# Running sums of the seven products in PSUM, with fewer VectorE additions and another order of items

## Chip, core and metric

The kernel runs on one core of a Trainium2 chip. The metric is the device time of one execution in microseconds (us). The engines are TensorE (PE, with its weight loads shown as PEld), VectorE (DVE), ScalarE (ACT), GpSimd (POOL) and SyncE (SP), which issues most of the DMAs.

## The reference

A decoder trunk of two layers on 256 rows of width 2048: each layer has an attention (differential attention in the first, multi-head latent attention in the second), a cross-attention into 256 memory rows, and an MLP with squared ReLU, each behind an RMSNorm and with a residual addition. One RMSNorm closes the trunk. The part that the change touches is the MLP:

```python
def sq_relu_mlp(h, wup, wdown):
    return jnp.square(jax.nn.relu(h @ wup)) @ wdown   # h 256 x 2048, wup 2048 x 8192, wdown 8192 x 2048

x = x + sq_relu_mlp(rms_norm(x, mlp_norm[i]), mlp_wup[i], mlp_wdown[i])
```

## The kernel before

**Products in halves.** Every float32 operand is split into a high half (a cast to float32r) and a low half (the rest). One product of the algorithm is three matmuls: high by high, high by low, low by high. Weights come from HBM as tiles `raw` of 128 x 2048 (1 MB, seven buffers). A tile is split in two steps of 128 x 1024: ScalarE casts the high half (`whi`, L199) and VectorE subtracts to get the low half (`wlo`, L200), with four buffers of each. TensorE's 128 x 512 matmuls (L157) take these as the moving operand.

**The MLP's items.** The hidden width 8192 is worked in eight blocks (b = 0 to 7) of 1024 columns. The 256 rows are two tiles of 128. Block 0 is multiplied straightforwardly: *up* items. The hidden activations (after ReLU, square and transposes) meet wdown in *down* items, whose sums stay in four PSUM banks. An up or down item is one weight tile with 24 matmuls.

Blocks 1 to 7 are multiplied as a 2 x 2 block product in seven products instead of eight (class `Seven`, Strassen's scheme). The 2 x 2 blocks are the two row tiles by the two halves of the inner width, and the two halves of the inner width by two groups of 512 columns. p1 to p7 each multiply one form of the activations (a quarter of it, or a running sum `s1`, `s2`, `s3`, `s4` of quarters) by one form of the weights. A product has two items (x = 0 and x = 1), each one weight tile with 12 matmuls, and sums into one PSUM bank, `pr`. The weight forms are made in place: additions of two raw tiles on VectorE (L824, at the items of p5, p6 and p2), and for p7 an accumulating DMA from GpSimd's queue (L816), which adds a tile from HBM onto p3's raw tile once p3's item has been split. p7's x-th item needs the tile that followed p3's x-th item.

**Combination before.** After the second item of each product its bank is read. p1 and p5 are copied to SBUF by ScalarE (L892). The others are combined by VectorE in SBUF (helper `add`, L886): p6 + p1; p3 + p5 and from that minus p6; p2 + p1; p7 onto p6 and p5 minus that; p4 onto p6. These are seven VectorE operations a block, five from PSUM and two within SBUF. Each of the four results goes to `out`: ReLU with the row's scale and square on ScalarE (L1212, L1213), then four transposes on TensorE (L161) through a side bank and a split into the hidden unit (L338, L339).

**What sets the order.** TensorE's instructions run in the order in which they are written. `mlp_line` writes it: it merges the list `rest` (up and down items) with the list `seven` by a running balance of estimated VectorE time (function `vector`) against TensorE time (1 for a Seven item, 2 for another), with share the ratio of the two sums; a Seven item is taken when the balance is at or below zero, or when the next down item's hidden units are not ready. Within a block `ORDER` gives the items. In blocks 5 to 7 the line before is p1 p1 p5 D p5 D p6 D p3 p6 D p3 p2 D D p7 p2 D p7 D p4 p4, with D for a down item; block 1 is p1 p1 p5 U p5 U p6 U p3 p6 U p3 p2 p7 p2 D D D p7 D D p4 p4, with U for an up item.

The other engines' instructions are ordered by a scheduler that works from estimated times and priorities at build time; `urgent()` raises a priority. Weight tiles are fetched up to four items ahead (`take`, `fill`), and the loads of p5, p6 and p2 one item earlier still (`fetch`). PSUM has eight banks in one pool.

Of the kernel before, what the change touches and what calls it, by code (L numbers as in the profile page):

```python
# [10 lines left out]
F32 = mybir.dt.float32  # L11
# [3 lines left out]
ALU = mybir.AluOpType  # L15
AX = mybir.AxisListType

P = 128
# [3 lines left out]
CH = 512  # L22
# [5 lines left out]
EVS = 7  # L28
# [19 lines left out]
def trunk(ctx, tc, x, xT, xT0, mem, memT, positions, gcols, gfinal, lam_vecs, consts, W, out):  # L48
    nc = tc.nc

    def pool(name, bufs, space=None):
        kw = {"space": space} if space else {}
        return ctx.enter_context(tc.tile_pool(name=name, bufs=bufs, **kw))
# [5 lines left out]
    work = pool("work", 2)  # L59
# [5 lines left out]
    def nm(s):  # L65
        serial[0] += 1
        return f"{s}_{serial[0]}"
# [4 lines left out]
    def bank(tag="ax"):  # L72
        return banks.tile([P, CH], F32, tag="bank", name=nm(tag))
# [38 lines left out]
    def pump():  # L112
        while True:
            now = [t for t in side if t.due() <= clock[0]]
            if not now:
                return
            min(now, key=lambda t: (t.ready, t.serial)).step()

    def need(tasks):
        for task in tasks:  # L120
            while not task.done:
                nxt = min(side, key=lambda t: (t.due(), t.serial))
                clock[0] = max(clock[0], nxt.due())
                nxt.step()
# [24 lines left out]
    def give_back():  # L149
        free_banks[0] += 1  # L150

    def mmul(o, stationary, moving, start, stop):
        n = 1
        for d in moving.shape[1:]:
            n *= d
        clock[0] += max(0.11, n / 2400 + 0.0133)
        return nc.tensor.matmul(o, stationary, moving, start=start, stop=stop)  # L157

    def flip(o, src):
        clock[0] += 0.109  # L160
# [5 lines left out]
    def urgent():  # L166

        return tc.high_priority(offset=URGENT)
# [58 lines left out]
    def take():  # L227
        fill()
        got = ready.pop(0)
        fill()  # L230
        taken[0] += 1
        if taken[0] in hooks:
            hooks[taken[0]]()
        return got

    def unit_part(o, a, h, hi, lo, t, first, last):

        width = o.shape[-1]
        for k in range(2):
            kk = 2 * h + k  # L240
            ah, al = a.get(0, kk, t), a.get(1, kk, t)
            wh = hi[:, k * width : (k + 1) * width]
            wl = lo[:, k * width : (k + 1) * width]
            mmul(o, ah, wh, first and kk == 0, False)
            mmul(o, ah, wl, False, False)
            mmul(o, al, wh, False, last and kk == 3)
        pump()
# [534 lines left out]
    class Chunk:  # L782
# [11 lines left out]
        def items(self):  # L794
            return [Item(self, u, [job]) for u, job in enumerate(self.all)]
# [5 lines left out]
    class Seven:  # L801

        ORDER = "p1 p1 p5 p5 p6 p3 p6 p3 p2 p7 p2 p7 p4 p4".split()
        A = {"p1": (0, 0), "p2": (0, 1), "p3": "s4", "p4": (1, 1), "p5": "s1", "p6": "s2", "p7": "s3"}

        def __init__(self, l, b):
# [54 lines left out]
        def items(self):  # L863
            order = [(p, self.ORDER[:i].count(p)) for i, p in enumerate(self.ORDER)]
            return [Item(self, u, [self.job(*u)]) for u in order]

        def products(self, a, u, copied, out):
            p, x = u
            form = a.form(self.A[p])
            need(form.tasks)  # L870
            if x == 0:
                self.banks[p] = bank("pr")
            o = self.banks[p]
            for h, (hi, lo) in enumerate(take()):
                for k in range(2):
                    kk = 4 * x + 2 * h + k
                    wh, wl = (w[:, k * CH : (k + 1) * CH] for w in (hi, lo))
                    mmul(o, form[:, 0, kk], wh, kk == 0, False)
                    mmul(o, form[:, 0, kk], wl, False, False)
                    mmul(o, form[:, 1, kk], wh, False, kk == 7)  # L880
                pump()
            if x == 0:
                return

            def add(o, p, q, op=ALU.add):
                nc.vector.tensor_tensor(o, p, q, op)  # L886

            c = copied
            if p in ("p1", "p5", "p6", "p3"):
                c[p] = work.tile([P, CH], F32, tag="ev", name=nm(p), bufs=EVS)  # L890
            if p in ("p1", "p5"):
                nc.scalar.copy(c[p], o)  # L892
            elif p == "p6":
                add(c[p], o, c["p1"])
            elif p == "p3":
                add(c[p], o, c["p5"])
                add(c[p], c[p], c["p6"], ALU.subtract)
                out(0, 1, c[p], c[p])
            elif p == "p2":
                add(c["p1"], o, c["p1"])  # L900
                out(0, 0, c["p1"], c["p1"])
            elif p == "p7":
                add(c["p6"], o, c["p6"])
                add(c["p5"], c["p5"], c["p6"], ALU.subtract)
                out(1, 1, c["p5"], c["p5"])
            else:
                add(c["p6"], o, c["p6"])
                out(1, 0, c["p6"], c["p6"])

    def mlp_line(l):  # L910

        def up(b, h):
            return Chunk(l, "up", [(b, h)]).items()

        def both(b, *more):
            return [(b, 0), (b, 1), *more]

        groups = [both(b) for b in range(MLP_BLOCKS)]  # L920

        def down(i):

            end = len(groups) - 1
            pairs = ((0, 1), (2, 3)) if (end - i) % 2 == 0 else ((2, 3), (0, 1))
            chunks = [Chunk(l, "down", groups[i], c, open=i == 0) for c in pairs[0]]
            chunks += [Chunk(l, "down", groups[i], c, close=i == end) for c in pairs[1]]
            return [i for c in chunks for i in c.items()]

        line = up(0, 0)  # L930
        rest = up(0, 1) + [i for b in range(MLP_BLOCKS - 1) for i in down(b)]
        seven = [i for b in SEVEN for i in Seven(l, b).items()]

        def vector(item):

            if isinstance(item.of, Seven):
                p, x = item.u
                return 1 + (p in ("p5", "p6", "p2")) + x * {"p6": 0.3, "p3": 0.9, "p2": 0.6, "p7": 0.9, "p4": 0.6}.get(p, 0)
            return 1 + 0.6 * (item.u == len(item.of.all) - 1 and item.of.close)

        def tensor(item):
            return 1 if isinstance(item.of, Seven) else 2

        rest, after = rest[:-3], rest[-3:]

        share = sum(map(vector, rest + seven)) / sum(map(tensor, rest + seven))
        usable = {(0, 0): 0}
        lead, now = 0.0, 0
        while rest or seven:
            of = rest[0].of if rest else None  # L950
            late = rest and of.kind == "down" and any(usable.get(h, math.inf) > now for h in of.halves)
            take_seven = seven and (not rest or late or lead <= 0)
            item = (seven if take_seven else rest).pop(0)
            lead += vector(item) - share * tensor(item)
            now += tensor(item)
            line.append(item)
            if isinstance(item.of, Seven):
                if item.u == ("p4", 1):
                    usable.update({(item.of.b, h): now + 6 for h in range(2)})
            elif item.of.kind == "up" and item.u == 3:  # L960
                usable[item.of.halves[0]] = now + 4
        return line + after, down(len(groups) - 1)
# [586 lines left out]
def build(a, w):  # L1549
    import concourse.bacc as bacc  # L1550

    nc = bacc.Bacc("TRN2", target_bir_lowering=False, num_devices=1, dynamic_dma_scratch_size=1024)
    arrays = {}

    def dram(name, v):
        arrays[f"in_{name}_dram"] = v
        return nc.dram_tensor(f"in_{name}_dram", v.shape, mybir.dt.from_np(v.dtype), kind="ExternalInput").ap()

    args = [dram(k, a[k]) for k in ("x", "xT", "xT0", "mem", "memT", "positions", "gcols", "gfinal", "lam_vecs", "consts")]
    weights = {k: dram(k, v) for k, v in w.items()}  # L1560
    o = nc.dram_tensor("out_0_dram", (S, D), F32, kind="ExternalOutput").ap()
    with tile.TileContext(nc, schedule_with_timeline_sim=True) as tc, tc.manual_schedule(engines={mybir.EngineType.PE}):
        trunk(tc, *args, weights, o)
    return nc, arrays
# [8 lines left out]
```

## Time and profile before

| | before |
|---|---|
| timed runs, median of 3 | 2216.66 us (2216.47 to 2217.68) |
| profiled execution, first to last instruction (its span) | 2214.3 us |
| the median of the timed runs above that span | 2.4 us |
| TensorE busy | 2201.7 us |
| VectorE busy | 1760.7 us |
| ScalarE busy | 1357.0 us |
| mean granted TensorE clock | 0.999 |

No time of its own is given for the profiled execution besides its span; the timed runs stand beside it. In rows of the profile L157 is line 157, the helper that writes every matmul, so rows are told apart by tiles: `mm` is the bank of an up or down item, `pr` that of a Seven item, `ax` a side bank of transposes. `out<-in` names the tile written and those read, xcount is the number of instructions, and a bracket at the end of a timeline row has the idle time of that engine just before the instruction and what ended it. "Busy, mean ns | idle before" are the columns of a group.

### The profile page before, as it was taken

The numbers are of one execution on the slowest core, as the hardware profiler recorded it, in microseconds if no ns is written. First come the engines' busy times: TensorE is split into PE (matmuls) and PEld (weight loads), VectorE is DVE, ScalarE is ACT, GpSimd is POOL, SyncE is SP. The second block draws the span as 40 slices with busy tenths as digits, with TensorE's granted clock in tenths as the row PEclk, the third lists the DMA queues.
The fourth block names the chain that finished last, engine by engine and source line by source line (L and its number), as shares of the span: only waits on it lengthen the run. The fifth ranks groups of instructions, "written<-read, shape, count | busy, mean of one in ns | idle before, by whom it ended". The sixth has DMA issues, their size and how long they took to land.

```text
span 2214.3 us, 27594 instructions
## 1 busy us (share of the span) xinstructions
PE 2201.7 (99%) x10559; PEld 1846.1 (83%) x10559; DVE 1760.7 (80%) x1961; ACT 1357.0 (61%) x1811; POOL 134.3 (6%) x222
## 2 busy tenths in 40 slices
PE   9999999999999999999999999999999999999998
PEld 7888888888888888888889988888888888888886
DVE  6665757779889889889765878778988998898874
ACT  7554546666666666666655755556766666666664
POOL 1111010000000000000000411000000000000001
PEclk9999999999999999999999999999999999999999
DMA  9446555436766766875845444634767667677681
GB/s 386 156 152 228 188 194 210 166 118 209 259 203 211 254 212 215 250 218 212 251 176 178 136 152 163 247 129 156 222 234 228 210 246 228 197 259 226 195 282 57
DMA packets 69683, 454.73 MB, mean 205 GB/s; under 512 B 7984, under 2 KB 8368, under 8 KB 17584
## 3 DMA queue, kind: packets, MB, share of 16 engines
q1 hardware_dynamic: 65232, 423.09, 53.6%
q0 software_dynamic: 4032, 29.36, 7.2%
q8 instruction: 82, 1.34, 0.2%
q10 hardware_dynamic: 288, 0.52, 0.1%
q14 instruction: 49, 0.40, 0.0%
HBM read 450.85 MB, written 2.10 MB: 205 GB/s over the span
## 4 chain that ended last, share of the span: by engine, by line
PE 93%; DVE 4%; issue 1%; ACT 1%; POOL 1%; DMA 1%; POOLq 0%; ACTq 0%; DVEq 0%
PE mm L157 65%; PE pr L157 23%; PE ax L157 2%; PE ax L161 2%; DVE wlo L200 2%; PE mm L161 1%; DVE raw L824 1%; DVE unit L440 0%; DVE raw L468 0%; POOL rs L382 0%; ACT whi L199 0%; DMA raw<-in_mlp_wup_dram 0%; DVE raw L451 0%; DMA raw<-in_da_wqkv_dram 0%; DVE x L496 0%
## 5 line engine op out<-in xcount | busy, mean ns | idle before, releaser
L199 ACT CAST whi<-raw 128x1024 fp32r<-128x1024 f32 (+2 forms) x962 | 1000.4, 1041 | 715.2 <-PE mm L157 590.6
L200 DVE TENSOR_TENSOR wlo<-raw,whi 128x1024 fp32r<-128x1024 f32 (+2 forms) x962 | 1147.8, 1209 | 344.9 <-ACT whi L199 329.6
L157 PE MATMUL mm<-whi,unit 128*128 128x512 f32 (+3 forms) x4416 | 1396.2, 388 | 0.4 <-ACT unit L370 0.4
L157 PEld LDWEIGHTS mm<-whi,unit 128*128 128x128 f32 x4416 | 825.2, 188 | 161.4 <-ACT unit L370 1.5
L157 PE MATMUL mm<-wlo,unit 128*128 128x512 f32 (+3 forms) x2208 | 851.5, 386 | 1.0 <-DVE wlo L200 1.0
L157 PE MATMUL pr<-whi,unit 128*128 128x512 f32 x1568 | 505.6, 391 | 0.0
L157 PEld LDWEIGHTS mm<-wlo,unit 128*128 128x128 f32 x2208 | 415.3, 188 | 79.2 <-DVE wlo L200 3.3
L157 PEld LDWEIGHTS pr<-whi,unit 128*128 128x128 f32 x1568 | 294.4, 188 | 61.0
L157 PE MATMUL pr<-wlo,unit 128*128 128x512 f32 x784 | 305.4, 390 | 0.6 <-DVE wlo L200 0.6
L824 DVE TENSOR_TENSOR raw<-raw,raw 128x2048 f32<-128x2048 f32 x84 | 192.1, 2287 | 26.1 <-DMA raw<-in_mlp_wup_dram 25.6
L157 PEld LDWEIGHTS pr<-wlo,unit 128*128 128x128 f32 x784 | 147.3, 188 | 31.5 <-DVE wlo L200 1.4
L496 DVE TENSOR_TENSOR x<-x,mm 128x512 f32<-128x512 f32 x152 | 100.3, 679 | 9.4 <-PE mm L157 9.0
L816 POOL DMA_DIRECT2D raw<-in_mlp_wup_dram x28 | 24.6, 879 | 1094.7 <-DVE wlo L200 1094.7
L382 POOL TENSOR_TENSOR rs<-rs,mhalf 128x1 f32<-128x1 f32 (+1 forms) x28 | 26.0, 932 | 649.3 <-DVE rs L381 649.3
L338 ACT CAST unit<-ax 128x512 fp32r<-128x512 f32 x64 | 37.2, 581 | 24.4 <-PE ax L161 24.4
L886 DVE TENSOR_TENSOR p<-pr,p 128x512 f32<-128x512 f32 x70 | 47.9, 684 | 2.6 <-PE pr L157 2.6
L157 PE MATMUL mm<-unit,whi 128*128 128x256 f32 x256 | 47.1, 285 | 0.1
L161 PE MATMUL ax<-identr,p 128*128 128x128 f32 x304 | 46.2, 272 | 0.5 <-ACT unit L1434 0.5
L161 PEld LDWEIGHTS ax<-identr,p 128*128 128x128 f32 x304 | 37.7, 139 | 10.8 <-ACT unit L1434 0.9
L1212 ACT ACTIVATE p<-p,r 128x512 f32<-128x512 f32 x56 | 40.3, 720 | 9.3 <-DVE p L886 9.2
L339 DVE TENSOR_TENSOR unit<-ax,unit 128x512 fp32r<-128x512 f32 x64 | 43.7, 683 | 1.6 <-ACT unit L338 1.1
L376 ACT ACTIVATE junk<-x 128x512 bf16<-128x512 f32 x56 | 35.2, 628 | 9.4 <-DVE x L496 8.4
(161 smaller groups left out, 1053.2 us busy)
## 6 DMA issues: line engine op xcount, KB each, us to landing
raw<-in_mlp_wup_dram SPq DMA_DIRECT2D x128, 1024.0 KB, 5.0
raw<-in_mlp_wdown_dram SPq DMA_DIRECT2D x128, 1024.0 KB, 5.1
raw<-in_da_wqkv_dram SPq DMA_DIRECT2D x45, 1024.0 KB, 7.3
raw<-in_mlp_wup_dram POOLq DMA_DIRECT2D x28, 1024.0 KB, 8.1
raw<-in_da_wo_dram SPq DMA_DIRECT2D x16, 1024.0 KB, 5.0
raw<-in_ca_wkv_dram SPq DMA_DIRECT2D x16, 1024.0 KB, 5.0
raw<-in_mla_wo_dram SPq DMA_DIRECT2D x16, 1024.0 KB, 5.2
raw<-in_ca_wq_dram SPq DMA_DIRECT2D x8, 1024.0 KB, 6.9
```

What stands on the lines that cost most here:

```text
L157: return nc.tensor.matmul(o, stationary, moving, start=start, stop=stop)
L161: nc.tensor.transpose(o, src, ident)
L199: nc.scalar.copy(hi, r)
L200: nc.vector.tensor_tensor(lo, r, f32(hi), ALU.subtract)
L338: nc.scalar.copy(hi, src)
L339: nc.vector.tensor_tensor(dst[:, 1, :n, t * P : (t + 1) * P], src, f32(hi), ALU.subtract)
L376: nc.scalar.activation(junk[:, : src.shape[1]], src, AF.Square, accum_out=acc)
L382: nc.gpsimd.tensor_tensor(r[:, :n], r[:, :n], mhalf.broadcast_to([P, n]), ALU.pow)
L496: nc.vector.tensor_tensor(xc, xc, ps, ALU.add)
L824: nc.vector.tensor_tensor(o, o, q, ALU.add)
L886: nc.vector.tensor_tensor(o, p, q, op)
L1212: nc.scalar.activation(r, src, AF.Relu, scale=rstd[t])
```

## The change

The products that share a sum are accumulated in one bank. p1, p6, p7 and p4 go onto p1's bank one after the other, p3 onto p5's, and p2 has its own. After p1, p5 and p6 ScalarE copies the running sum to SBUF, with raised priority. VectorE does three operations a block: the sum with p3 minus the copy made after p6, the copy of p5 minus the sum with p7 (with raised priority), and p2 plus the copy of p1. p4's result is read from PSUM by the ReLU. A matmul that goes onto a used bank does not start a new sum (`start` is false), and has to come after the reading of that bank's earlier sum.

In `ORDER` the last items of p2 and p7 change places: p2 p7 p7 p2 for p2 p7 p2 p7. The planner's estimates of VectorE's time (`vector`) get values for the three operations, which changes where down items are put among the Seven items.

```diff
-    def mmul(o, stationary, moving, start, stop):
+    def mmul(o, stationary, moving, start, stop, onto=False):
...
-        return nc.tensor.matmul(o, stationary, moving, start=start, stop=stop)
+        return nc.tensor.matmul(o, stationary, moving, start=start, stop=stop, skip_group_check=onto)
...
-        ORDER = "p1 p1 p5 p5 p6 p3 p6 p3 p2 p7 p2 p7 p4 p4".split()
+        ORDER = "p1 p1 p5 p5 p6 p3 p6 p3 p2 p7 p7 p2 p4 p4".split()
+        ONTO = {"p1": "p1", "p6": "p1", "p7": "p1", "p4": "p1", "p5": "p5", "p3": "p5", "p2": "p2"}
...
-            if x == 0:
+            onto = self.ONTO[p]
+            if x == 0 and onto == p:
                 self.banks[p] = bank("pr")
-            o = self.banks[p]
+            o = self.banks[onto]
...
-                    mmul(o, form[:, 0, kk], wh, kk == 0, False)
-                    mmul(o, form[:, 0, kk], wl, False, False)
-                    mmul(o, form[:, 1, kk], wh, False, kk == 7)
+                    mmul(o, form[:, 0, kk], wh, kk == 0 and onto == p, False, onto != p)
+                    mmul(o, form[:, 0, kk], wl, False, False, onto != p)
+                    mmul(o, form[:, 1, kk], wh, False, kk == 7, onto != p)
...
-            def add(o, p, q, op=ALU.add):
-                nc.vector.tensor_tensor(o, p, q, op)
+            def kept():
+                t = work.tile([P, CH], F32, tag="ev", name=nm(p), bufs=EVS)
+                with urgent():
+                    nc.scalar.copy(t, o)
+                return t

             c = copied
-            if p in ("p1", "p5", "p6", "p3"):
-                c[p] = work.tile([P, CH], F32, tag="ev", name=nm(p), bufs=EVS)
-            if p in ("p1", "p5"):
-                nc.scalar.copy(c[p], o)
-            elif p == "p6":
-                add(c[p], o, c["p1"])
+            if p in ("p1", "p5", "p6"):
+                c[p] = kept()
             elif p == "p3":
-                add(c[p], o, c["p5"])
-                add(c[p], c[p], c["p6"], ALU.subtract)
-                out(0, 1, c[p], c[p])
+                nc.vector.tensor_tensor(c["p6"], o, c["p6"], ALU.subtract)
+                out(0, 1, c["p6"], c["p6"])
+            elif p == "p7":
+                with urgent():
+                    nc.vector.tensor_tensor(c["p5"], c["p5"], o, ALU.subtract)
+                out(1, 1, c["p5"], c["p5"])
             elif p == "p2":
-                add(c["p1"], o, c["p1"])
+                nc.vector.tensor_tensor(c["p1"], o, c["p1"], ALU.add)
                 out(0, 0, c["p1"], c["p1"])
-            elif p == "p7":
-                add(c["p6"], o, c["p6"])
-                add(c["p5"], c["p5"], c["p6"], ALU.subtract)
-                out(1, 1, c["p5"], c["p5"])
             else:
-                add(c["p6"], o, c["p6"])
-                out(1, 0, c["p6"], c["p6"])
+                out(1, 0, o, work.tile([P, CH], F32, tag="ev", name=nm(p), bufs=EVS))
...
-                return 1 + (p in ("p5", "p6", "p2")) + x * {"p6": 0.3, "p3": 0.9, "p2": 0.6, "p7": 0.9, "p4": 0.6}.get(p, 0)
+                return 1 + (p in ("p5", "p6", "p2")) + x * {"p3": 0.6, "p2": 0.6, "p7": 0.6, "p4": 0.3}.get(p, 0)
```

## The prediction

> **What bounds the kernel now.** I read the page first, then the busy time by stretches, then the waits of TensorE (PE), and then the timeline around each wait that was left. The two MLPs lie roughly in the stretches 505 to 1175 us and 1540 to 2215 us.
>
> ```profile
> span 2214.3 us, 27594 instructions
> PE 2201.7 (99%) x10559; PEld 1846.1 (83%) x10559; DVE 1760.7 (80%) x1961; ACT 1357.0 (61%) x1811; POOL 134.3 (6%) x222
> ...
> 505.00:1175.00 670.00, 669.12 (x3027) 553.51 (x3026) 573.95 (x528) 425.81 (x477) 13.46 (x17) 1.00 0.68 221
> ...
> 1540.00:2215.00 675.00, 664.84 (x2990) 548.96 (x2988) 568.10 (x517) 421.51 (x470) 24.31 (x24) 1.00 0.66 215
> ```
>
> The rows of stretches give length, then busy time of PE, PEld, DVE (VectorE), ACT (ScalarE) and POOL. In the first MLP PE is busy for 669.12 of 670.00 us; VectorE, which the change relieves, for 573.95 (86%). A busy PE can still be a slow one, because ends of matmuls are modelled. So the pace comes from the chain of waits: one row of 24 products without a wait in it,
>
> ```profile
> 546.67 5.44 PE pr L157 x24
> ```
>
> 5.44 / 24 = 0.227 us for one 128x512 product, hence 2.72 us for one item of a Seven block (12 products) and 5.44 us for an up or down item (24). The change leaves the number of products as it is, so only the time that PE loses beyond this pace can be won. The waits view has it:
>
> ```profile
> PE mm L157 <- DVE wlo L200: 1.0, 3, 0.4
> PE pr L157 <- DVE wlo L200: 0.6, 2, 0.3
> ```
>
> Five waits, 1.6 us in all, in which PE wanted the low half of a weight from VectorE. All five are in the MLPs. PE's timeline has each of them, with the product before it:
>
> ```profile
> 529.46 0.39 PE L157 MATMUL pr<-whi,unit 128*128 128x512 f32 x1
> 530.14 0.50 PE L157 MATMUL pr<-wlo,unit 128*128 128x512 f32 x1 [0.29 <-DVE wlo L200]
> ...
> 614.22 0.39 PE L157 MATMUL mm<-whi,unit 128*128 128x512 f32 x1
> 615.01 0.50 PE L157 MATMUL mm<-wlo,unit 128*128 128x512 f32 x1 [0.41 <-DVE wlo L200]
> ...
> 823.83 0.50 PE L157 MATMUL mm<-wlo,unit 128*128 128x512 f32 x1 [0.18 <-DVE wlo L200]
> ...
> 1567.14 0.50 PE L157 MATMUL pr<-wlo,unit 128*128 128x512 f32 x1 [0.30 <-DVE wlo L200]
> ...
> 1652.00 0.50 PE L157 MATMUL mm<-wlo,unit 128*128 128x512 f32 x1 [0.40 <-DVE wlo L200]
> ```
>
> From start to start 614.22 to 615.01 is 0.79 us where 0.227 is the pace, so 0.56 is lost, and the next product runs 0.11 longer (0.50 against 0.39): 0.67 for an idle time of 0.41, or idle time plus 0.26. The five cost 1.58 + 5 x 0.26 = 2.9 us. This is all that a faster VectorE can give back, 0.13% of the span.
>
> [...]
>
> **What is removed and added.** Durations by tile, of the whole execution (14 Seven blocks):
>
> ```profile
> L886 DVE TENSOR_TENSOR p<-pr,p x70: 675/683/692, 554.8 to 2145.6; 128x512 f32<-128x512 f32 x70
> L886 DVE TENSOR_TENSOR p<-p,p x28: 681/682/685, 562.1 to 2136.0; 128x512 f32<-128x512 f32 x28
> ...
> L892 ACT COPY p<-pr x28: 569/574/584, 521.5 to 2079.5; 128x512 f32<-128x512 f32 x28
> ```
>
> VectorE did 98 operations, 7 a block; now 3 a block, 42. That is 56 x 0.683 = 38.2 us less, 19.1 an MLP. ScalarE copies p6 as well: 14 x 0.574 = 8.0 us more. The ReLU of p4 now reads PSUM instead of SBUF; I take it at no change. None of it is on PE, so its worth is what it does to the five waits and to new ones.
>
> *The three later waits* (615.01, 823.83, 1652.00) follow a stretch of short items, p4 p4 p1 p1 p5, where VectorE falls behind. It shows ahead of 615.01:
>
> ```profile
> 607.12 0.68 DVE L886 TENSOR_TENSOR p<-pr,p 128x512 f32<-128x512 f32 x1
> ...
> 611.53 2.29 DVE L824 TENSOR_TENSOR raw<-raw,raw 128x2048 f32<-128x2048 f32 x1
> 613.74 4.62 DVE L200 TENSOR_TENSOR wlo<-raw,whi 128x1024 fp32r<-128x1024 f32 x4
> ```
>
> The row of 607.12 is p4's addition, which is gone. The next operation starts 0.6 us after it (the last 0.08 overlap), so the split at 613.74 starts about 0.6 earlier, and 0.41 of wait goes: late next would be ScalarE's half, but those casts are done before. The same holds at 1652.00. The one at 823.83 followed a weight that VectorE waited for,
>
> ```profile
> 820.35 2.29 DVE L824 TENSOR_TENSOR raw<-raw,raw 128x2048 f32<-128x2048 f32 x1 [2.73 <-DMA raw<-in_mlp_wup_dram]
> ```
>
> and could stay; I take it as gone, since its p2 item is now two items later. Gain: 0.41 + 0.18 + 0.40 + 3 x 0.26 = 1.8 us; bounds 0 to 1.8. The two waits at 530.14 and 1567.14 come before the first addition that is removed (the first L886 is at 554.8) and stay.
>
> *New waits on PSUM.* p6, p7 and p4 now go onto p1's bank and p3 onto p5's, so PE must wait until ScalarE's copy (0.57 us), or for p4 VectorE's subtraction of p7 (0.68), has read the bank. Everything queued behind on PE waits too, since it is in order. What lies between follows from the order, for which I walked the planner's loop by hand with the new costs (VectorE's units per unit of PE fall from 1.081 to 1.041). Block 1 becomes p1 p1 p5 U p5 U p6 U p3 p6 U p3 p2 p7 p7 D D D p2 D D p4 p4, and blocks 2 to 7 p1 p1 p5 D p5 D p6 D p3 p6 D p3 p2 D D p7 p7 p2 D D p4 p4 (U up, D down). Between a copy and the product that waits for it are, at least: p1 to p6 p5, D, p5, D, 16.3 us; p5 to p3 D, p6, D, 13.6; p6 to p7 U, p3, p2 in block 1, 10.9; p7 to p4 p2, D, D, 13.6. Against 0.57 and 0.68, so I put these waits at nothing. The cover would have to fall by 10 us before one shows. Banks: four for the down sums, one for transposes, and at most three for products (an old one being read, p1, and p5 or p2) make eight, as before; bounds here 0 to one wait of 0.4 + 0.26 a block, 14 x 0.66 = 9.2 us.
>
> *The moved item.* p7's second item stands one item earlier (p2 p7 p7 p2 for p2 p7 p2 p7). Its weight is made by an accumulating DMA that POOL starts once VectorE has split p3's second item. In blocks 2 to 7 p2, D, D and p7 lie between the second items of p3 and p7, 16.3 us of PE. In block 1 it is p2 and p7 alone. There, in the first MLP:
>
> ```profile
> 554.77 0.68 DVE L886 TENSOR_TENSOR p<-pr,p 128x512 f32<-128x512 f32 x1
> 555.37 2.35 DVE L200 TENSOR_TENSOR wlo<-raw,whi 128x1024 fp32r<-128x1024 f32 x2
> ...
> 556.90 0.87 POOL L816 DMA_DIRECT2D raw<-in_mlp_wup_dram  x1 [10.22 <-DVE wlo L200]
> ...
> raw<-in_mlp_wup_dram POOLq DMA_DIRECT2D x1, 1024.0 KB, 8.7
> ...
> DMA to landing us min/median/max: 7.9/8.1/10.9
> ```
>
> This DMA (the row with 8.7 is its own) lands at 565.6. p6's addition at 554.77 goes, which lets the split and the DMA start 0.6 earlier: landing at 565.0. Then a cast and a subtraction of half an item are due:
>
> ```profile
> L199 ACT CAST whi<-raw 128x1024 fp32r<-128x1024 f32 x333 | 350.3, 1054 | 221.1 <-PE mm L157 166.6 <-PE pr L157 42.3 <-DVE wlo L200 8.9
> ...
> L200 DVE TENSOR_TENSOR wlo<-raw,whi 128x1024 fp32r<-128x1024 f32 x334 | 399.4, 1219 | 72.2 <-ACT whi L199 65.2
> ```
>
> 565.0 + 1.05 + 1.22 and about 0.1 for two handovers is 567.4. When does PE want it? It runs p3, p2, p7 from 557.39, with one group of transposes, and the third item after p3's starts with the second product of the pair below, its low half at 566.27:
>
> ```profile
> 557.39 0.39 PE L157 MATMUL pr<-whi,unit 128*128 128x512 f32 x1
> ...
> 565.82 0.62 PE L157 MATMUL pr<-whi,unit 128*128 128x512 f32 x2
> 566.27 0.39 PE L157 MATMUL pr<-wlo,unit 128*128 128x512 f32 x1
> ```
>
> That place was p2's and is p7's now. The product is late by 567.4 - 566.27 = 1.1 us, with 0.11 for the longer product after it 1.25 us. Down items follow at once and the split catches up on them (5.44 us of PE for 4 splits of 1.22), so nothing more is lost. The second MLP has the same order and the same DMA in its block 1: together 2.5 us. Bounds: with the trace's shortest landing, 7.9, 0.8 less each, 0.9 together; with the longest, 10.9, 2.2 more each, 6.9. I take the row of that very DMA.
>
> [...]
>
> **The sum.** -1.8 + 2.5 = +0.7 us on a span of 2214.3: 2215.0. The median of the timed runs (2216.66) lies 2.4 above the profiled span, so 2217.4 us.
>
> **The rivals.**
> *A, no new wait at p7.* The split of p3 in block 1 comes earlier than I think, or the landing is faster. For it: VectorE has less to do. Against: it has only one addition less before that place. 2216.66 - 1.8 = 2214.9.
> *B, the late landing (slower).* The DMA of block 1 lands at the trace's longest 10.9: PE loses 6.9 us over both MLPs, net +5.1, 2221.8. It decides from a loss of 3.1 us in each MLP, a landing some 10.6 us after the issue. For it: this DMA's 8.7 is already over the median. Against: 10.9 is the longest of all, the median 8.1.
> *C, copies in the way (slower).* The copies are urgent, and stand ahead of casts on ScalarE's queue; if one waits there for its product, the casts behind it wait too. At 0.66 us a block that is 9.2 us, net +7.4: 2224.1. Against: down items follow most copies, and ScalarE is idle for a third of the MLP.
> *D, PE has headroom (faster).* If VectorE's load set the 0.227 us, the 38.2 us taken off it would come back: 2178.5. Against it is the wait-free row of 24.
> *E, no effect.* Neither the old waits go nor a new one comes: 2216.7, within the same class as the forecast.
>
> **How the numbers follow.** 0.2% is 4.4 us, about what a measurement of this kernel can tell from no change. Forecast with its own spread (2215.5 to 2219) 0.55, A 0.13, E 0.10, B 0.11, C 0.08, D 0.03. Faster: D, 0.03. Same: forecast, A and E, 0.78. Slower: B and C, 0.19. The range leaves out D and most of C: from 2214.6, a little under A, to 2222.5, a little over B.
>
> **What would show it.** Right: PE's waits in block 1 of each MLP name ScalarE's cast, VectorE's split or the DMA at p7's second item, about 1 us each; no wait near the old 615 and 1652; L886's successors number 42 on VectorE and the copies 42 on ScalarE; PE's waits on copies are nil. Wrong: waits of PE that name a copy or the subtraction, a repeated wait in every block, or a pace of products other than 0.227 us.

## The result, and the profile after

| | before | changed |
|---|---|---|
| median, 10 runs each | 2216.87 us (2215.57 to 2217.70) | 2223.22 us (2220.07 to 2223.76) |
| ratio | | 1.0026, 95% interval 1.0017 to 1.0035 |
| span of the profiled execution | 2214.3 us | 2221.7 us |

The change makes the kernel slower by 0.26%. The forecast was 2217.4, with a range from 2214.6 to 2222.5.

The page, the waits of PE and one row of the chain of waits of the changed kernel, which answer to those shown of before (VectorE's additions of weights, L824 before, are now L825):

```profile
span 2221.7 us, 27569 instructions
PE 2204.2 (99%) x10559; PEld 1849.5 (83%) x10559; DVE 1730.0 (78%) x1905; ACT 1361.9 (61%) x1825; POOL 133.2 (6%) x222
...
PE pr L157 <- DVE wlo L200: 5.2, 4, 2.3
PE mm L157 <- DVE wlo L200: 0.3, 1, 0.3
...
640.74 5.44 PE pr L157 x24
```

VectorE is busy 30.7 us less and PE is no faster: 24 products without a wait still take 5.44 us. (The durations of the 56 operations do come to the 38.2 us of the prediction; but part of each overlapped its neighbour, and the splits, L200, take 2.7 us more in all than before.) PE's waits for low halves have grown from 1.6 us to 5.5. No wait of PE names a copy or a subtraction. The timeline of PE has the growth at two places, p7's second item of block 1 in each MLP; this is the first, and the one row of the second:

```profile
567.72 0.48 PE L157 MATMUL pr<-whi,unit 128*128 128x512 f32 x1
570.48 0.72 PE L157 MATMUL pr<-wlo,unit 128*128 128x512 f32 x1 [2.28 <-DVE wlo L200]
570.99 1.06 PE L157 MATMUL pr<-whi,unit 128*128 128x512 f32 x2
571.85 0.63 PE L157 MATMUL pr<-wlo,unit 128*128 128x512 f32 x1
...
1610.54 0.50 PE L157 MATMUL pr<-wlo,unit 128*128 128x512 f32 x1 [2.32 <-DVE wlo L200]
```

The wait is 2.3 us, and the products behind it run at 0.43 us from start to start, not 0.227. The stretches behind both waits (length, busy time of PE, PEld, DVE, ACT, POOL, then the granted clock, the DMA share and GB/s) say why: the granted clock was lowered, to 0.66 over 5 us.

```profile
570.00:575.00 5.00, 4.52 (x13) 3.60 (x14) 5.00 (x7) 1.05 (x1) 0.00 (x0) 0.66 0.70 224
...
1611.00:1616.00 5.00, 5.00 (x17) 3.67 (x16) 5.00 (x7) 1.05 (x1) 0.00 (x0) 0.66 0.92 290
```

I summed, over the two MLPs, what each start-to-start of two products exceeds 0.227 us by, where it does so by more than 0.09. Place by place, in us:

| place | before | changed |
|---|---|---|
| block 1, first wait (530 and 1567) | 0.67 + 0.67 | 0.68 + 0.67 |
| block 1, p7's second item | 0 | 4.22 + 4.29 |
| after p4 p4 p1 p1 p5 (615 and 1652) | 0.68 + 0.67 | 0 |
| at 824 before; at 1706 and 2124 after | 0.45 | 0.55 + 0.37 |
| sum | 3.1 | 10.8 |

The difference, 7.6 us, is that of the spans (7.4). Of 4.2 us at p7, some 2.5 are the wait and what goes with it, and 1.7 the low clock. The ten timed runs show the second part by itself: the two at 2220.1 us have a mean clock of 0.999, the eight others, 2221.7 to 2223.8, have 0.997 or 0.998.

**What VectorE did at that place.** VectorE's timeline in the changed kernel, and the additions' place in the kernel before:

```profile
547.75 5.31 DVE L200 TENSOR_TENSOR wlo<-raw,whi 128x1024 fp32r<-128x1024 f32 x4 [1.32 <-ACT whi L199]
...
564.24 1.23 DVE L200 TENSOR_TENSOR wlo<-raw,whi 128x1024 fp32r<-128x1024 f32 x1 [1.01 <-ACT whi L199]
567.00 2.29 DVE L825 TENSOR_TENSOR raw<-raw,raw 128x2048 f32<-128x2048 f32 x1 [1.53 <-DMA raw<-in_mlp_wup_dram]
569.21 1.22 DVE L200 TENSOR_TENSOR wlo<-raw,whi 128x1024 fp32r<-128x1024 f32 x1
```

```profile
550.30 2.28 DVE L824 TENSOR_TENSOR raw<-raw,raw 128x2048 f32<-128x2048 f32 x1
```

The split at 564.24 is p7's first half, the one at 569.21 its second. Between them stands the addition L825 that makes p4's weight out of p2's second weight tile. It waits 1.53 us for that tile's load and works 2.2 us, and p7's second half waits behind it. Before, the same addition was done at 550.30, ahead of p3's splits; now the row of 547.75 has four splits there, one behind the other. The rows of the two DMAs, POOL's (p7's weight) and SP's (p2's tile), each with its time to landing, and ScalarE's cast of p7's first half:

```profile
555.21 0.87 POOL L817 DMA_DIRECT2D raw<-in_mlp_wup_dram  x1 [8.54 <-DVE wlo L200]
...
raw<-in_mlp_wup_dram POOLq DMA_DIRECT2D x1, 1024.0 KB, 7.9
...
559.88 0.33 SPq L171 DMA_DIRECT2D raw<-in_mlp_wup_dram  x1
...
raw<-in_mlp_wup_dram SPq DMA_DIRECT2D x1, 1024.0 KB, 7.1
...
563.16 1.05 ACT L199 CAST whi<-raw 128x1024 fp32r<-128x1024 f32 x1 [0.94 <-DMA raw<-in_mlp_wup_dram]
```

p7's weight landed at 563.1, in good time: its first half was split at 565.5, and PE came to that half's first low product at 566.23. p2's tile was asked for at 559.88 only. The program writes such a load one step ahead of the item's own place in the list of weights; p2's second item now stands three down items later, so two down weights go ahead of it on SP's queue.

### The profile page after: what moved, and what is told of

Its sections match the earlier page's. It is cut to its first block, busy times and chain, and to the rows that moved or that the text cites. A ratio compares the mean times of both kernels' runs of the same rounds, so it can differ in the third digit from the quotient of the medians.

```text
span 2221.7 us, 27569 instructions
## 1 busy us (share of the span) xinstructions
PE 2204.2 (99%) x10559; PEld 1849.5 (83%) x10559; DVE 1730.0 (78%) x1905; ACT 1361.9 (61%) x1825; POOL 133.2 (6%) x222
## 4 chain that ended last, share of the span: by engine, by line
PE 92%; DVE 4%; DMA 2%; ACT 1%; issue 1%; POOL 0%; POOLq 0%; ACTq 0%; DVEq 0%
PE mm L157 64%; PE pr L157 22%; PE ax L157 2%; PE ax L161 2%; DVE wlo L200 2%; DMA raw<-in_mlp_wup_dram 1%; PE mm L161 1%; DVE raw L825 1%; ACT whi L199 0%; DVE unit L440 0%; DVE raw L468 0%; POOL rs L382 0%; DVE raw L451 0%; DMA raw<-in_da_wqkv_dram 0%; DVE x L496 0%
## 5 line engine op out<-in xcount | busy, mean ns | idle before, releaser
L200 DVE TENSOR_TENSOR wlo<-raw,whi 128x1024 fp32r<-128x1024 f32 (+2 forms) x962 | 1150.2, 1212 | 366.4 <-ACT whi L199 351.2
L825 DVE TENSOR_TENSOR raw<-raw,raw 128x2048 f32<-128x2048 f32 x84 | 192.3, 2289 | 48.0 <-DMA raw<-in_mlp_wup_dram 47.9
L161 PEld LDWEIGHTS ax<-identr,p 128*128 128x128 f32 x304 | 37.7, 139 | 10.8 <-ACT unit L1433 0.9
L157 PEld LDWEIGHTS mm<-unit,whi 128*128 128x128 f32 x256 | 40.0, 192 | 0.4 <-DVE unit L339 0.3
L157 PE MATMUL mm<-unit,wlo 128*128 128x256 f32 x128 | 36.3, 283 | 0.0
```

The source lines that it names most:

```text
L161: nc.tensor.transpose(o, src, ident)
L200: nc.vector.tensor_tensor(lo, r, f32(hi), ALU.subtract)
L825: nc.vector.tensor_tensor(o, o, q, ALU.add)
```

## Experiments

Three theories were set against one another. *Q*: the loss comes from VectorE's queue in block 1, as just read. *L*: it comes from the late landing of p7's accumulating DMA, as the prediction had it. *P*: the sums in PSUM cost the time. Each kernel was timed against the kernel before in five rounds. "Lost" is the sum over both MLPs as in the table above (3.1 before, 10.8 changed). Some edits add lines above the rows shown: in e3, e5 and e8 the split L200 is L202, and in e3 and e5 the addition L825 is L827.

| run | median, us | ratio to before, 95% | lost, us |
|---|---|---|---|
| e1_old_order | 2244.28 | 1.0121 (1.0107 to 1.0135) | 28.9 |
| e2_only_order | 2226.82 | 1.0047 (1.0034 to 1.0060) | 11.4 |
| e3_add_last | 2226.34 | 1.0042 (1.0029 to 1.0056) | 10.8 |
| e5_add_after_p7 | 2223.73 | 1.0031 (1.0020 to 1.0043) | 8.8 |
| e9_block1_old_order | 2216.51 | 0.9998 (0.9989 to 1.0007) | 2.9 |
| e8_block1_add_last | 2215.98 | 0.9998 (0.9989 to 1.0006) | 1.4 |
| e4_early_load | 2217.91 | 1.0007 (0.9998 to 1.0016) | 5.4 |

The first four are some 2 us slower than their losses say. In their profiled executions 1.4 to 1.7 us of it lie ahead of the MLPs, where the edits change nothing; e4's has 1.7 there too. I did not follow it up, and its cause stays open.

**The sums without the new order.**

```diff
-        ORDER = "p1 p1 p5 p5 p6 p3 p6 p3 p2 p7 p7 p2 p4 p4".split()
+        ORDER = "p1 p1 p5 p5 p6 p3 p6 p3 p2 p7 p2 p7 p4 p4".split()
```

> The changed kernel with the old order of items (p2 p7 p2 p7), everything else of the change kept: sums in PSUM, copies, three VectorE operations. Theory Q (VectorE's queue: in block 1 the addition of p2's second weight stands between the two halves of p7's second weight and waits for its load): no wait of 2 us on PE in block 1, clock stays full, time 2215 to 2216.9. Theory P (the sums in PSUM cost the time, by waits on copies and banks): stays at 2220 to 2224. Theory L (p7's accumulating DMA lands too late for the item's new place, as predicted): 2215 to 2216.9 like Q, so this run does not part Q from L.

It was far slower than any of the three had expected. The waits of PE, one of them on its timeline, and the clock behind two of them:

```profile
PE pr L157 <- DVE p L901: 19.1, 10, 2.2
...
PE pr L157 <- DVE wlo L200: 0.6, 2, 0.3
...
943.76 0.47 PE L157 MATMUL pr<-whi,unit 128*128 128x512 f32 x1 [1.85 <-DVE p L901]
...
770.00:775.00 5.00, 4.18 (x11) 3.31 (x12) 2.11 (x4) 2.45 (x4) 0.00 (x0) 0.66 0.88 315
857.00:862.00 5.00, 3.91 (x17) 3.28 (x18) 3.25 (x4) 3.60 (x5) 0.00 (x0) 1.00 0.75 283
```

The waits at p7's second item of block 1 are gone, as Q and L said. But with the new estimates and the old order the planner's line ends blocks 3 to 7 with p7 p4 p4, nothing between. p4 goes onto the bank that the subtraction of p7 (L901) has to read first, so PE waits some 1.9 us, once in each of ten blocks. The subtraction itself takes 0.68 us; ahead of it on VectorE (at 943.76) splits and another subtraction had to end first. So with this planner the sums in PSUM need the new order in those blocks: it puts p2 and two down items between p7 and p4. (The old estimates had a down item there in blocks 5 to 7; the sums with the old order and the old estimates were not run.) The wait that the prediction put at nothing is nothing because of that cover.

**The new order without the sums.** The diff is on the kernel before: the same line of `ORDER`, the other way round.

> The kernel before with only the order of items changed (p2 p7 p7 p2); the seven VectorE operations and the seven banks stay. Q and L: a wait of PE of 2 to 2.5 us at p7's second item of block 1 in the first MLP and likely in the second, with the clock lowered for some 4 us behind it: 2220 to 2225. P: 2216 to 2218, as before. The queue of VectorE has the addition between p7's halves here too (Q: PE's wait begins at the second half's low product, not the first's).

```profile
PE pr L157 <- DVE wlo L200: 3.8, 4, 1.6
PE mm L157 <- DVE wlo L200: 3.2, 8, 0.4
```

The wait at p7's second item of block 1 is there in both MLPs, 1.6 us, and as Q said it begins at the second half's low product, with seven additions a block and no sum shared: the order brings it, not the sums. It is shorter than the 2 to 2.5 us expected, and the clock stayed full, at 1.00, behind it in the profiled execution (of the timed runs the slowest, 2228.95, has a mean clock of 0.997). The time lies above the expected 2220 to 2225 all the same, since the second row was not foreseen: eight waits of 0.4 us in blocks 2 to 5, which the changed kernel does not have. The first of them in each MLP (at 619 and 1660) stands behind the same line of items as in the changed kernel, so the line did not remove it there; nor did the long wait ahead of it, since e8 has neither the long wait nor this one. From block 2 to block 4 the two lines differ, and in the later blocks, where they agree again, e2 has no such wait; what part the fewer operations and what part the line have in the other six was not tested.

**p2's additions last, in all blocks.**

```diff
                 elif p == "p2":
                     o = r.pop((21, x))
-                    add(r["t", x], o)
+                    split = halves_of(o)
+                    with tc.issue_after(low[0].ins):
+                        add(r["t", x], o)
+                    return split
```

`low[0]`, set in lines left out here, is the latest subtraction of a low half that has been written.

> The changed kernel, new order kept, with each addition of p2 (L825, weights) tied behind the split of p2's own weight on VectorE's queue; loads and the accumulating DMA are untouched. Q: the 2.3 us waits of block 1 go and with them the low clock: 2215 to 2216.9. L: the waits stay, 2220 to 2224. P: the waits stay or others show, 2220 to 2224.

```profile
PE pr L157 <- DVE wlo L202: 1.0, 4, 0.3
```

The wait of 2.3 us at p7's second item is gone and the clock stayed full (mean 0.999, as before), with the code of the loads and DMAs untouched; that speaks for Q and against L. Of the four waits two are those at block 1's beginning, and two, of 0.22 us, stand at p7's first item, behind the addition of p2's first weight, which is tied as well. The time was a miss: in blocks 2 to 7, 24 new losses of 0.35 us arise, 8.4 in all.

**p2's second addition behind p7's second half.**

```diff
                 elif p == "p7":
-                    o = r.pop((22, x))
+                    split = halves_of(r.pop((22, x)))
+                    self.p7_low = low[0]
+                    return split
                 elif p == "p2":
                     o = r.pop((21, x))
-                    add(r["t", x], o)
+                    if x:
+                        with tc.issue_after(self.p7_low.ins):
+                            add(r["t", x], o)
+                    else:
+                        add(r["t", x], o)
```

> The changed kernel with the addition of p2's second weight tied only behind p7's second half, so that it now stands ahead of the next down item's halves. Q: p7's wait goes; the down item's first low half is late instead, by 567.0 (landing) + 2.2 + 1.2 + 0.06 - 569.5 = about 1 us of idle time in each MLP; if the clock falls only after a longer idle time, it stays full: 2217 to 2219. L: the wait at p7 stays at about 2.3 us, 2220 to 2224.

```profile
568.79 2.29 DVE L827 TENSOR_TENSOR raw<-raw,raw 128x2048 f32<-128x2048 f32 x1
...
572.87 0.50 PE L157 MATMUL mm<-wlo,unit 128*128 128x512 f32 x1 [1.56 <-DVE wlo L202]
```

The wait followed the addition: p7 is free, and the next down item waits 1.56 us (1.61 in the second MLP), more than the 1 us expected. The clock stayed full, at 1.00 behind both waits. Twelve losses of 0.32 us in other blocks came with the tie, so the time missed the expected 2217 to 2219 as well.

**The old order in block 1 alone.**

```diff
-            order = [(p, self.ORDER[:i].count(p)) for i, p in enumerate(self.ORDER)]
+            names = list(self.ORDER)
+            if self.b == 1:
+                names[10:12] = names[11:9:-1]
+            order = [(p, names[:i].count(p)) for i, p in enumerate(names)]
```

> The changed kernel with the old order (p2 p7 p2 p7) in block 1 of each MLP alone; blocks 2 to 7 keep the new order. Theory Q (the loss lies in block 1 alone, where the new order sets the addition of p2's second weight between p7's halves): both waits of 2.3 us go, and the low clock behind them: what PE loses over its pace in the MLPs falls from 10.8 to about 2.3 us, against 3.1 before, time 2215 to 2217. Theory L (p7's DMA lands too late): the same. Theory P (sums in PSUM cost time in every block): 2220 or more.

```profile
PE mm L157 <- DVE wlo L200: 0.8, 2, 0.5
...
PE pr L157 <- DVE wlo L200: 0.6, 2, 0.3
```

What the change cost was in block 1: with two items exchanged in two of fourteen blocks the kernel is level with before, within 0.1%.

**p2's second addition last, in block 1 alone.** The edit of e3 under `if self.b == 1 and x:`.

> The changed kernel with the new order everywhere; in block 1 alone the addition of p2's second weight is tied behind the split of p2's own weight on VectorE's queue. Loads and the accumulating DMA are as in the changed kernel. Q: PE's wait at p7's second item falls from 2.3 us to 0.3 or less, clock full, 2215 to 2217. L: the wait stays near 2.3 us, 2220 to 2224. That addition and the next block's first one now stand side by side later on, which may cost a wait of 0.4 us.

```profile
PE pr L157 <- DVE wlo L202: 0.6, 2, 0.3
...
564.65 1.23 DVE L202 TENSOR_TENSOR wlo<-raw,whi 128x1024 fp32r<-128x1024 f32 x1 [1.04 <-ACT whi L201]
566.12 1.23 DVE L202 TENSOR_TENSOR wlo<-raw,whi 128x1024 fp32r<-128x1024 f32 x1 [0.24 <-ACT whi L201]
```

p7's two halves now follow each other, and the only waits for weights left in both MLPs are the two at block 1's beginning. Q is shown: same order, same loads, same DMA (ScalarE's cast of p7's first half, which waits for the landing, starts at 563.57, in the changed kernel at 563.16), and the wait and the low clock are gone (mean clock 0.999). It loses 1.8 us less than the kernel before, and its median lies 0.4 us under it; the interval reaches from 0.9989 to 1.0006, so it is not shown to be faster.

**p2's second load earlier, in block 1 alone.**

```diff
                 elif p == "p7":
                     o = r.pop((22, x))
+                    if self.b == 1 and x == 0:
+                        r[21, 1] = self.fetch(1, 0, 1)
```

> The changed kernel with the new order everywhere; in block 1 alone the load of p2's second weight is issued one item earlier, with p7's first item, so that the addition stands ahead of p7's splits on VectorE's queue and has its operands. Q: no wait over 0.5 us at p7's second item, clock full, 2215 to 2217.5. L: the accumulating DMA is where it was, so the wait stays near 2.3 us, 2220 to 2224.

```profile
552.03 2.28 DVE L825 TENSOR_TENSOR raw<-raw,raw 128x2048 f32<-128x2048 f32 x1
...
558.03 0.87 POOL L817 DMA_DIRECT2D raw<-in_mlp_wup_dram  x1 [9.57 <-DVE wlo L200]
...
566.94 1.05 ACT L199 CAST whi<-raw 128x1024 fp32r<-128x1024 f32 x1 [2.95 <-DMA raw<-in_mlp_wup_dram]
...
569.30 0.50 PE L157 MATMUL pr<-wlo,unit 128*128 128x512 f32 x1 [0.76 <-DVE wlo L200]
```

Now the addition has its operands and goes first, ahead of p3's split, as in the kernel before. The two long waits go, as Q said. But p3's split is then later, so is p7's DMA, and at p7's first half PE waits 0.76 us (0.59 in the second MLP) for a weight that has just landed; Q had no wait over 0.5 us, and the time is a little over its range. This is the predicted mechanism, L, on the VectorE order that the prediction had assumed: p7's item loses 1.41 and 0.87 us, where the prediction had 1.25 each. It is real, and in the changed kernel it did not arise, because there the DMA starts earlier (555.21 against 558.03).

## Why the prediction was wrong

**Right.** PE bounds the kernel, and no VectorE time was to be had beyond the waits: 30.7 us off VectorE's busy time left the pace of 0.227 us as it was, which also disposes of rival D. The three later waits went (615, 824, 1652); two smaller ones took their place at 1706 and 2124, where the sum had none. They are of the kind of 824: at both, an addition L825 had first waited about 4 us for its load. The order worked out by hand is the one that the trace has, and the waits on banks are nil; e1 shows that this rested on the cover: with nothing between p7 and p4 the same wait costs some 1.9 us a block. C did not come true: the 42 copies waited at most 0.3 us for their products, and no wait of PE in the MLPs names a cast or a copy.

**The step that failed** is the one on the moved item. Its place was right, block 1 of each MLP at p7's second item, and its sign; its cause and its size were wrong. I followed p7's weight and forgot what else moves with the exchange: p2's second item goes three down items later, its load goes with it on SP's queue, and with the load the addition that reads it, from 550.30 to 567.00 on VectorE. That had two effects. The addition was no longer ahead of p3's splits, so p7's DMA started 1.7 us earlier (555.21 against 556.90), not 0.6, and its weight was in time. And it came to stand between p7's halves and held the second for 3.7 us. The predicted 1.25 us in each MLP became 2.5. That the place and the sign came out right is luck: the late landing from which they were worked out did not happen.

**The term that was missing** is the clock: the prediction kept the pace of 0.227 us behind a wait without saying why, and it cost 1.7 us in each MLP in the profiled execution, on top of the wait. The two timed runs at 2220.1, whose mean clock is 0.999 as before, show what is left without it: 2.7 us over the forecast. With 2 x (2.5 + 1.7) in place of 2.5, the sum -1.8 + 2.5 becomes -1.8 + 8.4 + 0.9 (the two new small waits) = +7.5, against 7.4 in the spans. The ratio of the timed runs, 1.0026, is 5.8 us.

Rival B had the right sign, place and nearly the price (2221.8), by luck too: the landing took 7.9 us, not 10.9.

## What to carry to other kernels

When two items change places, list every instruction and every load that belongs to each of them, and find its new neighbours on the queue of its engine; the item that moves back can hurt more than the one that moves forward (here p2's addition cost 2.28 us of idle time on PE, p7's landing none). An operation that waits for a load can hold up what stands behind it on its engine (here 1.53 us of waiting and 2.2 of work on VectorE became those 2.28 us), so look at its place as well as at its length. In this kernel, with PE at its pace, 30.7 us less on VectorE could win only the waits that can be named, 1.6 us of idle time before. And the accumulation onto a used bank was free with p2 and two down items between the reader and the next writer, and cost some 1.9 us a block in e1 with nothing between.

## What was not expected of the hardware

In the changed kernel two waits of PE cost nearly twice their length: 2.28 and 2.32 us of idle time, 4.22 and 4.29 us lost. Behind them the granted clock was 0.66 over a stretch of 5 us and products took 0.43 us. In e1, of ten waits (19.1 us in all, the longest 2.2) four were followed by a lowered clock (0.66 to 0.72 in the stretches behind them) and six were not (1.00). Behind the waits of 1.6 us in e2 and e5, two in each, it stayed at 1.00 in the profiled executions.

Each of the two lowerings in the MLPs of the changed kernel is a stretch of 3.41 us at 0.50, which by itself costs 1.7 us. Here are the first of them and the stretches of 3.41 us before it, which has the wait, and behind it, then the second:

```profile
567.18:570.59 3.41, 1.13 (x8) 0.72 (x7) 3.41 (x3) 2.30 (x3) 0.00 (x0) 1.00 0.44 185
570.59:574.00 3.41, 3.41 (x9) 2.67 (x10) 3.41 (x4) 1.05 (x1) 0.00 (x0) 0.50 0.75 240
574.00:577.41 3.41, 3.41 (x18) 2.84 (x17) 2.81 (x5) 1.13 (x2) 0.00 (x0) 1.00 0.95 363
...
1611.66:1615.07 3.41, 3.41 (x10) 2.38 (x9) 3.41 (x5) 1.05 (x1) 0.00 (x0) 0.50 0.84 303
```

What parts the four waits of e1 from the other six was not shown, and no run was made to test it.
